# Softplus by absolute value, and the input projections of an attention mixer placed between the quarters of an S5 block

## The chip, the cores and the metric

The kernel runs on one core of one Trainium2 chip. Time is device microseconds of one execution; three runs of the kernel before took 2621.91, 2622.28 and 2622.65 us, and the median of 2622.28 us is what the changed kernel is measured against. One more execution was profiled.

## The reference

Two layers of a streaming encoder are run for 512 prompt rows and 128 sample rows (8 streams of 16 rows), 640 rows of 1024 channels in all. Each layer is FFN, mixer, FFN, each with a LayerNorm. The change lies in the first layer's mixer alone, which joins an S5 state space model with stick-breaking attention:

```python
def sb_block(q_blk, q_pos, k, v):
    z = jnp.einsum('bqhd,bkhd->bhqk', q_blk, k).astype(jnp.float32) * (SB_HEAD_DIM ** -0.5)
    mask = k_pos[None, :] < q_pos[:, None]
    sp = jnp.where(mask, jax.nn.softplus(z), 0.0)
    suffix = lax.cumsum(sp, axis=3, reverse=True) - sp
    w = jnp.where(mask, jnp.exp(jax.nn.log_sigmoid(z) - suffix), 0.0)
    return jnp.einsum('bhqk,bkhd->bqhd', w, v)
...
    proj = x @ w_in              # u | q | k | v, 512 columns each
    ys, h_last = s5_recurrence(u, h0, a_bar, b_bar, c_mat)
    g = jax.nn.gelu(ys + d_skip * u)
    s5_out = g * jax.nn.sigmoid(g @ w_glu + b_glu)
    sb_out = stick_breaking(q, k_all, v_all, offset)
    out = jnp.concatenate([s5_out, sb_out], axis=-1) @ w_out
```

There are 8 heads of 64 channels. The kernel writes k and v and the last S5 state out as well.

## The kernel before

All matrix products of weights run on TensorE (PE) as three products of a value split in a high and a low part (`mm3`, L119). `load_w` brings 512 KB of weights through SyncE's (SP's) queue into one of 4 raw tiles and splits them into two of 11 weight units: ScalarE (ACT) casts (L86), VectorE (DVE) subtracts (L87).

The instructions of each engine stand in a fixed order, which a planner makes when the kernel is built: from the order of the code, from what depends on what, and from when tiles and PSUM banks come free. Each engine takes its list in order and waits at the head of it.

`mixer0` goes like this:

- u is projected for all 640 rows (L119), then four S5 quarters follow, `s5_quarter(j)`. Each is one chain: PE transposes u (L657, L664), multiplies with `m2` (L672) and `tt` (L726); DVE rotates and scans (L680 to L720); PE multiplies the states with `et` (L731), ACT copies `yt` (L733), PE transposes back (L739), DVE copies `y` (L740), then ACT and DVE make the gelu (L743 to L749).
- v is projected (5 row tiles of 24 matmuls of 512 columns). The planner placed these 120 matmuls into the gaps of the four quarters.
- The PSUM banks and the working tiles are handed over from the S5 to attention. DVE and GpSimd (POOL) build the masks (`negc` L795, `negs`).
- `in_qk(p)` projects q and k of a pair of heads p: 4 groups of 24 matmuls, two of 256 and two of 384 columns.
- For each of four pairs, `attend(p, i, ...)` works on block i of the prompt (128 queries against 128(i+1) keys), and `sample(p, ...)` on the 128 sample rows in two halves f. Both go: matmuls to scores z in PSUM, mask added by PE (L837, L882), softplus (L823 to L826), a scan along the keys (L842, L887), z minus the scan (L844, L889), exponential, transposes on PE (L849, L893), a copy (L850, L894), matmuls with v (L853, L902, L906). The result of a pair's prompt blocks is copied at L938, that of its sample block at L916.
- Scores have two PSUM buffers (`bank_z`); `sample` takes one of them, and shares its bank `"o"` and the single tiles `kk`, `tm`, `kc` with the next sample.
- Beside attention stand the projections of pairs 2 and 3, the gate `wglu`, and the first half of the output projection (`out_half(0, t)`, 120 matmuls, accumulated by DVE at L775). The second half, `out_half(4, t)`, needs the last pair and ends the mixer with the LayerNorm.

Of the kernel before, what the change touches and what calls it, by code (L numbers as in the profile page):

```python
# [9 lines left out]
F32 = mybir.dt.float32  # L10
F32R = mybir.dt.float32r
BF16 = mybir.dt.bfloat16
AF = mybir.ActivationFunctionType
ALU = mybir.AluOpType
# [7 lines left out]
T = 640  # L22
TP = 512
NT = 5
KT = 8
NF = 22
HALVES = ((0, 256), (256, 384))
# [8 lines left out]
def kernel(ctx: ExitStack, tc: tile.TileContext, I, O, phases=PHASES):  # L36
    nc = tc.nc

    def pool(name, bufs=1, stack=ctx, **kw):
        return stack.enter_context(tc.tile_pool(name=name, bufs=bufs, **kw))  # L40
# [13 lines left out]
    def bank(k):  # L54
        return pools[k].tile([128, 512], F32, name="bank")

    def bank_a():
        return bank("a")
# [12 lines left out]
    def act_fn(out, in_, func, **kw):  # L71
        if state["preload"] is not None and func in (AF.Exp, AF.Ln):
            with tc.issue_after(state["preload"]):
                return nc.scalar.activation(out, in_, func, **kw)
        return nc.scalar.activation(out, in_, func, **kw)
# [9 lines left out]
    def split(hi, lo, src):  # L85
        nc.scalar.copy(hi, src)  # L86
        return nc.vector.tensor_tensor(lo, src, hi.bitcast(F32), op=ALU.subtract)  # L87

    def raw_tile():
        return pools["raw"].tile([128, 1024], F32, name="raw")  # L90

    def unit(dt=F32R, w=512):
        return pools["w"].tile([128, 1024 // w, w], dt, name="w")

    def load_w(src):

        r = raw_tile()
        nc.sync.dma_start(r, src)
        u = []
        for j in range(2):  # L100
            u.append(unit())
            split(u[j][:, 0], u[j][:, 1], r[:, 512 * j:512 * j + 512])
        return u

    def w_k(w, k):

        c = slice(k % 4 * 128, k % 4 * 128 + 128)
        return w[k // 4][:, 0, c], w[k // 4][:, 1, c]

    def w_j(w, j):  # L110

        return w[j][:, 0], w[j][:, 1]

    def mm3(ps, lhs, rhs):
        n = 3 * len(lhs)
        k = 0
        for (wh, wl), (xh, xl) in zip(lhs, rhs):
            for a, b in ((wh, xh), (wl, xh), (wh, xl)):
                state["pe"] = nc.tensor.matmul(ps, a, b, start=(k == 0), stop=(k == n - 1)).ins  # L119
                k += 1  # L120
# [5 lines left out]
    def cm_proj(w, h, nk=KT, src=None):  # L126
        o, L = HALVES[h]
        s = src or xt
        ps = bank_a()
        mm3(ps[:, :L],  # L130
            [w_k(w, k) for k in range(nk)],
            [(s["hi"][:, k, o:o + L], s["lo"][:, k, o:o + L]) for k in range(nk)])
        return ps
# [464 lines left out]
    def mixer0(ph, last):  # L598
        preload("natural_log_exp_and_others")
        V = nc.vector  # L600
        ctx_m = ExitStack()
        xh, xl = xt["hi"], xt["lo"]
        keep = pool("m0_keep", 1, ctx_m, reuse_waits="tile")
        g_ = [keep.tile([128, T], F32, name=f"g{m}") for m in range(4)]
        vt = keep.tile([128, NT, 512], F32, name="vt")
# [6 lines left out]
        def sigmoid_(t):  # L612

            act_fn(t, t, AF.Ln, bias=1.0)
            act_fn(t, t, AF.Exp, scale=-1.0)


        with ExitStack() as st:
            wk = pool("m0_s5", 1, st, reuse_waits="tile")
# [128 lines left out]
                sigmoid_(g)  # L748
                V.tensor_tensor(g_[j], g, y, op=ALU.mult)  # L749

            for j in range(4):
                s5_quarter(j)


            wv = [load_w(I["m0_v"][i]) for i in range(4)]
            for t in range(NT):
                pv = bank_a()
                mm3(pv, [(xh[:, k, t * 128:t * 128 + 128], xl[:, k, t * 128:t * 128 + 128]) for k in range(KT)],
                    [w_j(wv[k // 2], k % 2) for k in range(KT)])
                nc.scalar.copy(vt[:, t, :], pv)  # L760
                nc.sync.dma_start(O["v"][t * 128:t * 128 + 128, :], vt[:, t, :])
            for r in range(2):
                nc.sync.dma_start(O["s5"][r], fin[:, r])

# [12 lines left out]
        with ExitStack() as st:  # L777
# [42 lines left out]
            nc.scalar.copy(vrev, pr)  # L820

            def softplus_(e, z):
                V.tensor_scalar_min(e, z, 40.0)  # L823
                act_fn(e, e, AF.Exp)
                act_fn(e, e, AF.Ln, bias=1.0)
                V.tensor_tensor(e, z, e, op=ALU.max)  # L826

            def attend(p, i, qT, kT, po):

                n = 128 * i + 128  # L830
                z = bank_z()
                for h in range(2):
                    rows = slice(64 * h, 64 * h + 64)
                    nc.tensor.matmul(z[:, h, :n], qT[rows, n - 128:n], kT[rows, :n],
                                     start=True, stop=False, skip_group_check=True)
                for h in range(2):
                    nc.tensor.matmul(z[:, h, n - 128:n], identb, negc, start=False, stop=True, skip_group_check=True)  # L837
                e = wk.tile([128, 2, 512], F32, name="es", bufs=4)
                S = wk.tile([128, 2, 512], F32, name="S", bufs=2)
                softplus_(e[:, :, :n], z[:, :, :n])  # L840
                for h in range(2):
                    V.tensor_tensor_scan(S[:, h, :n][:, ::-1], onec[:, 0:1].to_broadcast([128, n]),  # L842
                                         e[:, h, :n][:, ::-1], 0.0, op0=ALU.mult, op1=ALU.add)
                V.tensor_tensor(S[:, :, :n], z[:, :, :n], S[:, :, :n], op=ALU.subtract)  # L844
                act_fn(S[:, :, :n], S[:, :, :n], AF.Exp)

                for h in range(2):
                    for j in range(i + 1):
                        nc.tensor.transpose(z[:, h, 128 * j:128 * j + 128], S[:, h, 128 * j:128 * j + 128], ident)  # L849
                nc.scalar.copy(e[:, :, :n], z[:, :, :n])  # L850
                for j in range(i + 1):
                    for h in range(2):
                        nc.tensor.matmul(po[64 * h:64 * h + 64, n - 128:n],  # L853
                                         vt[:, j, 128 * p + 64 * h:128 * p + 64 * h + 64],
                                         e[:, h, 128 * j:128 * j + 128],
                                         start=(j == 0), stop=(j == i), skip_group_check=True)
# [60 lines left out]

            onec = wk.tile([128, 1], F32, name="onec", bufs=1)
            V.memset(onec, 1.0)
            qk = {}  # L920

            def in_qk(p):
                for n, sc in (("q", 0.125), ("k", 1.0)):
                    wt = load_w(I["m0_in"][4 + 2 * p + "qk".index(n)])
                    t = qk[p, n] = keep.tile([128, T], F32, name=n + "T", bufs=4 if n == "q" else 3)
                    for h in range(2):
                        o, L = HALVES[h]
                        nc.scalar.mul(t[:, o:o + L], cm_proj(wt, h)[:, :L], sc)
                nc.sync.dma_start(O["kT"][128 * p:128 * p + 128, :], qk[p, "k"])

            in_qk(0)
            in_qk(1)
            for p in range(4):
                qT, kT = qk[p, "q"], qk[p, "k"]
                po = bank("o")
                for i in range(4):
                    attend(p, i, qT, kT, po)
                V.tensor_copy(qT[:, 0:512], po)  # L938
                sample(p, qT, kT)
                if p < 2:  # L940
                    in_qk(p + 2)
                if p == 1:
                    for m in range(4):
                        split(xh[:, m, :], xl[:, m, :], g_[m])
                    split(xh[:, 4, :], xl[:, 4, :], qk[0, "q"])
                if p:
                    split(xh[:, 4 + p, :], xl[:, 4 + p, :], qT)
# [3 lines left out]
            for h in range(2):  # L951
                o, L = HALVES[h]
# [458 lines left out]
    for ph in phases:  # L1411
        last = ph == phases[-1]
        if ph.startswith("ffn"):
            ffn(int(ph[3]), ph, last, sides.get(ph))
        elif ph == "mix0":
            mixer0(ph, last)
        else:
            mixer1(ph, last)
            if "ffn3" not in phases:
                with ExitStack() as st:  # L1420
                    psum(st, "ssd", a=4, b=4)
                    for _ in ssd_states(pool("ssd", 1, st, reuse_waits="tile")):
                        pass
# [111 lines left out]
```

## Time and profile before

| what | value |
|---|---|
| median of three runs | 2622.28 us |
| the profiled execution, its span | 2621.98 us, 2619.8 us |
| PE busy | 2552.1 us (97%), 15673 matmuls |
| DVE busy | 2028.7 us (77%) |
| ACT busy | 1149.4 us (44%) |
| POOL busy | 238.7 us (9%) |
| mixer 0, from the first S5 transpose to the end of the last sample block | 482.9 to 752.6 us |

Busy PE time holds the latency of pipelined matmuls and is no measure of how full PE is; the waits and the starts of the instructions are. Times in rows of the timeline are microseconds from the start of the span: start, busy time, engine, line, operation, output<-inputs, shape and count; in brackets the idle time of the engine before the row, and what ended it. Rows of groups have count | busy us, mean ns of one | idle before, releaser. Rows of a stretch give its length, then busy time (and count) of PE, of its weight loads, of DVE, ACT and POOL, the granted clock of PE as a share, the share of DMA and GB/s.

### The profile page before, as it was taken

How to read it: one execution, taken by the hardware profiler on the slowest of the kernel's cores; microseconds unless marked ns; L12 is line 12 of the kernel's file. 1: busy time of each engine (PE TensorE's matmuls, PEld its weight loads, DVE VectorE, ACT ScalarE, POOL GpSimd, SP SyncE). 2: the span in 40 equal slices, each digit the busy share in tenths (PEclk: the TensorE clock that was granted, in tenths of full speed). 3: DMA queues.
4: the chain of work that ended last, by engine and by line, in shares of the span. 5: the costliest groups of instructions: out<-in, count | busy, mean ns of one | idle time of the engine just before them, and what ended most of it. 6: DMA issues, size and time to landing. Idle time of an engine off the chain costs nothing. (4 is left out here: it accounts for less than half of the span.)

```text
span 2619.8 us, 41379 instructions
## 1 busy us (share of the span) xinstructions
PE 2552.1 (97%) x15673; PEld 2314.7 (88%) x15673; DVE 2028.7 (77%) x4074; ACT 1149.4 (44%) x2400; POOL 238.7 (9%) x356
## 2 busy tenths in 40 slices
PE   9999999999879999999999999999999999999998
PEld 8999999887559999998999999889989878998887
DVE  8898888657858777767976677777776789887778
ACT  4444444346524344333433343566565553343332
POOL 0000003010030000003000001311111150000001
PEclk9999999999979999999999999999999999999999
DMA  5333234542302233222122222356564622443432
GB/s 180 97 113 100 95 118 138 175 137 91 105 29 65 81 97 97 74 88 81 65 85 88 71 97 99 109 181 183 171 204 131 223 87 94 153 150 125 130 127 91
DMA packets 165751, 302.79 MB, mean 116 GB/s; under 512 B 19072, under 2 KB 89856, under 8 KB 165040
## 3 DMA queue, kind: packets, MB, share of 16 engines
q1 hardware_dynamic: 163792, 293.83, 35.0%
q0 software_dynamic: 1760, 6.33, 0.7%
q8 instruction: 123, 2.02, 0.3%
q14 instruction: 76, 0.62, 0.1%
HBM read 259.56 MB, written 40.54 MB: 115 GB/s over the span
## 5 line engine op out<-in xcount | busy, mean ns | idle before, releaser
L119 PE MATMUL bank<-w,h 128*128 128x512 f32 x2640 | 610.7, 391 | 0.0
L119 PEld LDWEIGHTS bank<-w,h 128*128 128x128 f32 x2640 | 492.3, 188 | 105.3 <-issue 3.4
L119 PE MATMUL bank<-xhi,w 128*128 128x256 f32 (+2 forms) x2528 | 560.4, 313 | 17.9 <-ACT w L86 6.3
L87 DVE TENSOR_TENSOR w<-raw,w 128x512 fp32r<-128x512 f32 x693 | 474.1, 696 | 101.4 <-ACT w L86 99.3
L334 PE MATMUL bank<-xhi,w 128*128 128x320 f32 x2432 | 539.8, 309 | 0.5 <-DVE w L87 0.3
L86 ACT CAST w<-raw 128x512 fp32r<-128x512 f32 x693 | 422.2, 620 | 260.0 <-PE bank L334 131.9
L119 PEld LDWEIGHTS bank<-xhi,w 128*128 128x128 f32 x2528 | 425.0, 190 | 30.7 <-ACT xhi L86 8.5
L334 PE MATMUL bank<-T,w 128*128 128x320 f32 x2736 | 425.1, 309 | 0.0
L334 PEld LDWEIGHTS bank<-xhi,w 128*128 128x128 f32 x2432 | 406.2, 188 | 6.4 <-issue 4.4
L334 PEld LDWEIGHTS bank<-T,w 128*128 128x128 f32 x2736 | 406.5, 188 | 0.0
L119 PE MATMUL bank<-xlo,w 128*128 128x256 f32 (+2 forms) x1264 | 393.4, 312 | 1.8 <-DVE xlo L87 1.8
L334 PE MATMUL bank<-xlo,w 128*128 128x320 f32 x1216 | 375.3, 309 | 0.0
L86 ACT CAST w<-sw 128x512 fp32r<-128x512 f32 x228 | 138.1, 620 | 463.2 <-PE bank L119 275.5
L196 DVE SCALAR_TENSOR_TENSOR yacc<-bank,yacc 128x512 f32<-128x512 f32 x240 | 164.8, 688 | 214.4 <-PE bank L119 212.9
L119 PEld LDWEIGHTS bank<-xlo,w 128*128 128x128 f32 x1264 | 240.8, 191 | 3.4 <-DVE xlo L87 2.4
L334 PEld LDWEIGHTS bank<-xlo,w 128*128 128x128 f32 x1216 | 228.0, 187 | 0.0
L87 DVE TENSOR_TENSOR w<-sw,w 128x512 fp32r<-128x512 f32 x228 | 156.1, 685 | 11.4 <-ACT w L86 11.0
L144 POOL DMA_DIRECT2D w<-in_ln_gb_dram x12 | 6.9, 578 | 1244.1 <-DVE h L87 1224.5
L119 PE MATMUL bank<-w,og 128*128 128x512 f32 x432 | 104.9, 396 | 1.4 <-DVE og L1331 1.2
L119 PEld LDWEIGHTS bank<-w,og 128*128 128x128 f32 x432 | 79.5, 188 | 19.2 <-DVE og L1331 3.1
L86 ACT CAST h<-hf 128x320 fp32r<-128x320 f32 x160 | 73.3, 459 | 49.4 <-DVE hf L371 45.9
L119 PE MATMUL bank<-w,xhi 128*128 128x512 f32 x240 | 83.7, 414 | 1.1 <-DVE yacc L775 1.1
(392 smaller groups left out, 2872.5 us busy)
## 6 DMA issues: line engine op xcount, KB each, us to landing
raw<-in_w_gate_dram SPq DMA_DIRECT2D x88, 512.0 KB, 3.7
raw<-in_w_up_dram SPq DMA_DIRECT2D x88, 512.0 KB, 3.7
raw<-in_w_down_dram SPq DMA_DIRECT2D x88, 512.0 KB, 4.1
raw<-in_m_in_dram SPq DMA_DIRECT2D x52, 512.0 KB, 3.7
raw<-in_m_out_dram SPq DMA_DIRECT2D x24, 512.0 KB, 3.7
csb<-cs_d SPq DMA_DIRECT2D x20, 512.0 KB, 5.2
h<-in_ssd_h_dram SPq DMA_DIRECT2D x16, 512.0 KB, 5.4
h<-in_ssd_h_dram SPq DMA_DIRECT2D x32, 256.0 KB, 2.7
```

The lines of the kernel that those rows point to most:

```text
L86: nc.scalar.copy(hi, src)
L87: return nc.vector.tensor_tensor(lo, src, hi.bitcast(F32), op=ALU.subtract)
L119: state["pe"] = nc.tensor.matmul(ps, a, b, start=(k == 0), stop=(k == n - 1)).ins
L144: nc.gpsimd.dma_start(g_bc[j], bass.AP(tensor=I["ln_gb"].tensor, offset=I["ln_gb"].offset + (2 * n + j) * D, ap=[[0, 128], [1, D]]))
L196: state["acc"] = nc.vector.scalar_tensor_tensor(ya, pb, scale, ya, op0=ALU.mult, op1=ALU.add).ins
L334: nc.tensor.matmul(ps, A[p][:, a, k * 128:k * 128 + 128], B[p][b][:, k, :], start=(first and n == 0), stop=(n == 11), skip_group_check=True)
```

## The change

Softplus was ln(1 + exp(min(z, 40))) and a maximum with z: DVE, ACT, ACT, DVE. It becomes max(z, 0) + ln(1 + exp(-|z|)): ACT three times, then one DVE instruction with two operations.

`in_qk` moves up, and the code now calls q and k of pair 0 after S5 quarter 0, v after quarter 1, q and k of pair 1 after quarter 2. In the last pair `sample` is called ahead of the prompt blocks.

```diff
+            def v_in():
+                wv = [load_w(I["m0_v"][i]) for i in range(4)]
+                ...
+            s5_quarter(0)
+            in_qk(0)
+            s5_quarter(1)
+            v_in()
+            s5_quarter(2)
+            in_qk(1)
+            s5_quarter(3)
-            for j in range(4):
-                s5_quarter(j)
-            wv = [load_w(I["m0_v"][i]) for i in range(4)]
-            ...
             def softplus_(e, z):
-                V.tensor_scalar_min(e, z, 40.0)
-                act_fn(e, e, AF.Exp)
+                nc.scalar.activation(e, z, AF.Abs)
+                act_fn(e, e, AF.Exp, scale=-1.0)
                 act_fn(e, e, AF.Ln, bias=1.0)
-                V.tensor_tensor(e, z, e, op=ALU.max)
+                V.scalar_tensor_tensor(e, z, 0.0, e, op0=ALU.max, op1=ALU.add)
...
-            in_qk(0)
-            in_qk(1)
             for p in range(4):
                 qT, kT = qk[p, "q"], qk[p, "k"]
+                if p == 3:
+                    sample(p, qT, kT)
                 po = bank("o")
                 for i in range(4):
                     attend(p, i, qT, kT, po)
                 V.tensor_copy(qT[:, 0:512], po)
-                sample(p, qT, kT)
+                if p < 3:
+                    sample(p, qT, kT)
```

The order on PE at the last S5 quarter, first before. Rows of L119 are v's projection, L657 and L664 the quarter's transposes, L672 the product with `m2`:

```order
L657 MATMUL bank<-ident,g_4888 80x128 x8
L119 MATMUL bank<-w,xhi 128x512
L119 MATMUL bank<-w,xlo 128x512
L119 MATMUL bank<-w,xhi 128x512 x2
L119 MATMUL bank<-w,xlo 128x512
L119 MATMUL bank<-w,xhi 128x512
L664 MATMUL bank<-ident,ut 128x80 x8
L119 MATMUL bank<-w,xhi 128x512
L119 MATMUL bank<-w,xlo 128x512
L119 MATMUL bank<-w,xhi 128x512
L672 MATMUL bank<-uc,m_5599 64x80 x8
```

The same place now, with the lines of the changed file (L668 for L657, and so on to L750 for L739; L852 is the first score matmul of pair 0, L119 is now q of pair 2):

```order
L668 MATMUL bank<-ident,g_4888 80x128 x8
L675 MATMUL bank<-ident,ut 128x80 x8
L683 MATMUL bank<-uc,m_6012 64x80 x16
L737 MATMUL bank<-tt,uc 80x128 x8
L742 MATMUL bank<-et,hr 80x256 x2
L742 MATMUL bank<-et,hi 80x256
L742 MATMUL bank<-et,hr 80x256
L742 MATMUL bank<-et,hi 80x256 x2
L742 MATMUL bank<-et,hr 80x256
L742 MATMUL bank<-et,hi 80x256
L750 MATMUL bank<-ident,yt 128x80 x8
L852 MATMUL bank<-kT,qT 128x128 x2
```

Nothing of another step stands in the last quarter any more. Behind quarter 0 now stand 59 matmuls of q and k of pair 0 beside the 37 in it, behind quarter 1 96 of v beside 24, behind quarter 2 62 of pair 1 beside 34.

The order on ACT at the first blocks of pair 0, before (L928 copies a projected group, L86 casts weights; `es` are softplus, `S` the exponential, L850 the copy of the transposes):

```order
L928 ACTIVATE kT<-bank 128x384
L86 CAST w<-raw 128x512
L74 ACTIVATE es<-es 128x2x128 x2
L74 ACTIVATE es<-es 128x2x256 x2
L74 ACTIVATE S<-S 128x2x128
L850 COPY es<-bank 128x2x128
```

The same place now (L841 is the absolute value, L625 copies a projected group, L837 is the copy of `vrev`):

```order
L837 COPY vrev<-bank 128x512
L841 ACTIVATE es<-bank 128x2x128
L841 ACTIVATE es<-bank 128x2x256
L74 ACTIVATE es<-es 128x2x128
L74 ACTIVATE es<-es 128x2x256
L74 ACTIVATE es<-es 128x2x128
L74 ACTIVATE es<-es 128x2x256
L625 ACTIVATE qT<-bank 128x384
L86 CAST w<-raw 128x512
L74 ACTIVATE S<-S 128x2x128
```

The two blocks' passes on ACT are now interleaved, three each.

The order on PE at the end of attention, before: the last blocks of pair 3 (L849, L853), then the last sample block from L867 on.

```order
L849 MATMUL bank<-ident,S 128x128 x6
L853 MATMUL bank<-es,vt 64x128 x6
L849 MATMUL bank<-ident,S 128x128 x8
L853 MATMUL bank<-es,vt 64x128 x8
L867 MATMUL bank<-ident,kT 128x128
L870 MATMUL bank<-anti,kk 128x128
L881 MATMUL bank<-kk,qb 128x128
L882 LDWEIGHTS identb
L882 MATMUL bank<-negs,identb 128x128
L884 MATMUL bank<-kc,qb 32x256 x4
```

Now, from the last projection that stands in attention (L119, `out_half(0)`): the end of sample block 2 (L911 to L930), the start of sample block 3 (L885 to L902) and the first scores of pair 3 (L852).

```order
L119 MATMUL bank<-w,xhi 128x512
L911 MATMUL bank<-ident,es 128x128 x3
L920 MATMUL bank<-vrev,tm 128x128
L924 MATMUL bank<-vc,tm 32x128 x8
L930 MATMUL bank<-ident,tm 128x128 x2
L885 MATMUL bank<-ident,kT 128x128
L888 MATMUL bank<-anti,kk 128x128
L899 MATMUL bank<-kk,qb 128x128
L900 LDWEIGHTS identb
L900 MATMUL bank<-negs,identb 128x128
L902 MATMUL bank<-kc,qb 32x256 x4
L852 MATMUL bank<-kT,qT 128x128 x2
```

Sample block 3 stands ahead of pair 3's prompt blocks, beside their first two, and pair 3's last blocks end the list, ahead of the second half of the output projection. No projection stands in pair 3.

More of the change, by code (lines that the diff above doesn't have):

```diff
@@ L615, in sigmoid_, with in_qk @@
             act_fn(t, t, AF.Exp, scale=-1.0)
+        qk = {}
+        def in_qk(p):
+            for n, sc in (("q", 0.125), ("k", 1.0)):
+                wt = load_w(I["m0_in"][4 + 2 * p + "qk".index(n)])
+                t = qk[p, n] = keep.tile([128, T], F32, name=n + "T", bufs=4 if n == "q" else 3)
+                for h in range(2):
+                    o, L = HALVES[h]
+                    nc.scalar.mul(t[:, o:o + L], cm_proj(wt, h)[:, :L], sc)
+            nc.sync.dma_start(O["kT"][128 * p:128 * p + 128, :], qk[p, "k"])
         with ExitStack() as st:
@@ L749, in s5_quarter @@
                 V.tensor_tensor(g_[j], g, y, op=ALU.mult)
-            for j in range(4):
-                s5_quarter(j)
-            wv = [load_w(I["m0_v"][i]) for i in range(4)]
[L756 to L761, printed above, removed]
+            def v_in():
+                wv = [load_w(I["m0_v"][i]) for i in range(4)]
+                for t in range(NT):
+                    pv = bank_a()
+                    mm3(pv, [(xh[:, k, t * 128:t * 128 + 128], xl[:, k, t * 128:t * 128 + 128]) for k in range(KT)],
+                        [w_j(wv[k // 2], k % 2) for k in range(KT)])
+                    nc.scalar.copy(vt[:, t, :], pv)
+                    nc.sync.dma_start(O["v"][t * 128:t * 128 + 128, :], vt[:, t, :])
+            s5_quarter(0)
[5 more added lines that the diff above has]
+            s5_quarter(3)
             for r in range(2):
@@ L919, in mixer0 @@
             V.memset(onec, 1.0)
[L920 to L929, printed above, removed]
-            in_qk(0)
-            in_qk(1)
             for p in range(4):
                 qT, kT = qk[p, "q"], qk[p, "k"]
+                if p == 3:
+                    sample(p, qT, kT)
                 po = bank("o")
```

## The prediction

> **What bounds the kernel now.** I read first the page's slices (its row of granted clock falls below 9 in one place alone, at 720 to 786 us, inside mixer 0), then mixer 0 by stretches, then its timeline engine by engine. The stretches are: the four S5 quarters; q and k of pairs 0 and 1; pair 0's attention; three periods that each run from one pair's copy of its result (L938) to the next; the last sample block.
>
> ```profile
> core 0: us, PE busy (x) PEld busy (x) DVE busy (x) ACT busy (x) POOL busy (x), PEclk, DMA share, GB/s
> 482.88:550.60 67.72, 66.00 (x481) 51.17 (x480) 52.92 (x166) 25.91 (x43) 2.48 (x13) 1.00 0.46 151
> 550.60:578.20 27.60, 27.60 (x188) 26.90 (x186) 9.82 (x21) 10.64 (x20) 6.95 (x22) 1.00 0.52 155
> 578.20:604.16 25.96, 23.75 (x180) 19.36 (x180) 17.85 (x24) 15.21 (x24) 0.00 (x0) 1.00 0.21 63
> 604.16:645.80 41.64, 38.37 (x309) 31.13 (x310) 31.18 (x50) 25.55 (x48) 0.58 (x2) 1.00 0.31 99
> 645.80:686.43 40.63, 37.73 (x254) 26.90 (x253) 36.26 (x63) 28.45 (x54) 0.58 (x2) 1.00 0.25 79
> 686.43:728.88 42.45, 33.62 (x213) 22.15 (x213) 29.41 (x46) 18.92 (x32) 1.76 (x4) 0.85 0.36 112
> 728.88:752.60 23.72, 13.08 (x75) 7.63 (x76) 8.43 (x14) 4.76 (x10) 0.00 (x0) 0.57 0.11 34
> ```
>
> PE is dense and at full clock until about 710 us because projections fill the gaps of attention; at the end nothing fills them, PE is busy 13.08 of 23.72 us and the clock is 0.57. No engine is full in the attention periods (DVE comes closest, 36.26 of 40.63), so they are chains: matmul, softplus, scans, exponential, transposes, copy, matmul. What counts is how long those chains are and what PE does beside them. The rest of the kernel keeps its instructions; I give it no change.
>
> **The change, part by part.** The sum goes from the first S5 transpose (482.88) to the first matmul of the dense output projection (749.93).
>
> (1) *S5.* The rows of one quarter, of the gelu behind the last quarter with the mask behind it, and of the projection rates:
>
> ```profile
> 482.88 1.04 PE L657 MATMUL bank<-ident,g 128*80 128x128 f32 x8
> 497.38 0.72 PE L739 MATMUL bank<-ident,yt 80*128 80x80 f32 x8
> 497.94 1.04 PE L657 MATMUL bank<-ident,g 128*80 128x128 f32 x8
> 549.90 1.39 DVE L740 COPY y<-bank 128x320 f32<-128x320 f32 x2
> 557.99 0.22 DVE L795 CAST negc<-mk 128x128 bf16<-128x128 f32 x1
> 567.30 0.39 ACT L928 ACTIVATE qT<-bank 128x256 f32<-128x256 f32 x1 [1.72 <-PE bank L119]
> 571.46 0.49 ACT L928 ACTIVATE qT<-bank 128x384 f32<-128x384 f32 x1 [1.46 <-PE bank L119]
> 574.18 0.39 ACT L928 ACTIVATE kT<-bank 128x256 f32<-128x256 f32 x1 [1.72 <-PE bank L119]
> 578.98 0.42 DVE L823 TENSOR_SCALAR es<-bank 128x256 f32<-128x256 f32 x1 [1.38 <-PE bank L837]
> 690.43 0.71 PE L119 MATMUL bank<-w,xhi 128*128 128x512 f32 x2
> 694.65 0.63 PE L119 MATMUL bank<-w,xhi 128*128 128x512 f32 x2
> ```
>
> A quarter takes 15.06 us (482.88 to 497.94). 24 matmuls of 384 columns take 4.16 us, of 256 columns 2.72, and one of 512 columns 0.234 (18 start between 690.43 and 694.65). By the order, quarter 0 now holds 37 of pair 0's 96 matmuls and 35 of 384 and 24 of 256 columns stand behind it: 6.1 + 2.7 = 8.8 us. Quarter 1 holds 24 of v's 120, 96 follow: 22.5 us. Quarter 2 holds 34 of pair 1's, 38 and 24 follow: 6.6 + 2.7 = 9.3. Quarter 3 holds none. So the S5 ends at 482.88 + 4 x 15.06 + 8.8 + 22.5 + 9.3 = 583.7. Then the first pair needs its mask, which stands on DVE behind the gelu: 549.90 to 558.21 before, less 0.7 us for a weight split and a qT copy that stood between, 7.6 us from the first y copy, itself 0.3 us ahead of the quarter's end. That is 591.0. Beside it PE has 36 matmuls of pair 2 (4.8 us) and little else. Before, the mask was built under q and k of pairs 0 and 1 (27.6 us, PE full), and the first softplus came at 578.98: **+12.0 us**. Weight loads and splits are as many as before and move with their matmuls; in DVE's and SP's order none stands ahead of quarter 3's work but one kT store and two loads whose buffers are free by then, so I cost them at nothing, covered by the projections behind quarters 0 to 2. Bounds: a bare quarter may be 0.5 us shorter (-2), or be like the mean of four before, 67.72/4 = 16.9 (+7.5).
>
> (2) *Softplus.* 24 passes of DVE (L823) become 24 of ACT:
>
> ```profile
> L823 DVE TENSOR_SCALAR es<-bank 128x384 f32<-128x384 f32 x8 | 4.5, 558 | 13.8 <-PE bank L884 13.8
> L823 DVE TENSOR_SCALAR es<-bank 128x1024 f32<-128x1024 f32 x4 | 4.9, 1218 | 0.3 <-PE bank L837 0.3
> L823 DVE TENSOR_SCALAR es<-bank 128x768 f32<-128x768 f32 x4 | 3.8, 956 | 3.1 <-PE bank L837 3.0
> L823 DVE TENSOR_SCALAR es<-bank 128x512 f32<-128x512 f32 x4 | 2.7, 678 | 0.0
> L826 DVE TENSOR_TENSOR es<-bank,es 128x512 f32<-128x512 f32 x4 | 2.7, 682 | 0.3 <-ACT es L74 0.3
> L196 DVE SCALAR_TENSOR_TENSOR yacc<-bank,yacc 128x512 f32<-128x512 f32 x240 | 164.8, 688 | 214.4 <-PE bank L119 212.9
> L74 ACT ACTIVATE es<-es 128x1024 f32<-128x1024 f32 x8 | 8.5, 1058 | 1.2 <-DVE es L823 1.1
> L74 ACT ACTIVATE es<-es 128x768 f32<-128x768 f32 x8 | 6.7, 843 | 2.9 <-DVE es L823 2.8
> L74 ACT ACTIVATE es<-es 128x512 f32<-128x512 f32 x8 | 5.0, 631 | 2.7 <-DVE es L823 2.2 <-DMA raw<-in_m_out_dram 0.4
> L850 ACT COPY es<-bank 128x1024 f32<-128x1024 f32 x4 | 4.1, 1015 | 4.4 <-PE bank L849 4.4
> 586.38 0.96 DVE L823 TENSOR_SCALAR es<-bank 128x768 f32<-128x768 f32 x1 [1.52 <-PE bank L837]
> 627.41 0.96 DVE L823 TENSOR_SCALAR es<-bank 128x768 f32<-128x768 f32 x1 [1.51 <-PE bank L837]
> 669.15 0.95 DVE L823 TENSOR_SCALAR es<-bank 128x768 f32<-128x768 f32 x1
> ```
>
> DVE loses 4.5 + 4.9 + 3.8 + 2.7 us and four of 0.42 (the 578.98 row): 17.6 us, 4.4 a pair. Abs from PSUM is not in the trace; its bounds are the PSUM copy (1.015) and the old DVE pass (1.218), and I take Exp's 1.058, the same engine and form. The last pass keeps its length: a two-operation add from PSUM (L196, 688 ns) takes what L826 takes (682). So a block still waits for three elementwise steps before its scans, and what counts is who queues behind whom.
>
> Pair 0, from its first pass to that of block 2: 7.40 us before (578.98 to 586.38). ACT now makes Abs, Exp and Ln of block 0 and Abs and Exp of block 1 first, some 3 x 0.42 + 2 x 0.63 = 2.5 us, before DVE can begin; so far ACT worked on block 0 while DVE made block 1's first pass. The rest follows in the old order, since block 2's mask stands on PE behind block 1's transposes; worked to the end it comes to 9.3: +1.9. From there to the pair's copy (17.8, to 604.16) DVE's order had block 3's pass (1.22) between block 2's last pass and its scans; that goes, and 0.96 becomes 0.84: -1.3. **Pair 0: +0.6.** In pairs 1 and 2 the second half (18.4 from 627.41, 16.65 + 0.6 from 669.15) loses the same 1.3. Their first half, with a sample block in it, gains length where ACT is late: casts of g, waiting for the last projections, stand ahead of the sample's last Exp in pair 1 (+0.4), and wglu's exponentials between the passes in pair 2 (+0.9). **-0.9 and -0.4.** Bounds of each: 3 us less, 2 more.
>
> (3) *The last sample block ahead of the last attention.*
>
> ```profile
> 686.43 0.69 DVE L938 COPY qT<-bank 128x512 f32<-128x512 f32 x1 [0.36 <-PE bank L853]
> 690.05 1.03 DVE L823 TENSOR_SCALAR es<-bank 128x384 f32<-128x384 f32 x2 [2.93 <-PE bank L884]
> 708.75 0.96 DVE L823 TENSOR_SCALAR es<-bank 128x768 f32<-128x768 f32 x1
> 728.88 0.69 DVE L938 COPY qT<-bank 128x512 f32<-128x512 f32 x1 [6.24 <-PE bank L853]
> 733.65 0.56 DVE L823 TENSOR_SCALAR es<-bank 128x384 f32<-128x384 f32 x1 [4.08 <-PE bank L884]
> 741.64 0.56 DVE L823 TENSOR_SCALAR es<-bank 128x384 f32<-128x384 f32 x1 [2.04 <-PE bank L884]
> 749.93 0.78 PE L119 MATMUL bank<-w,xhi 128*128 128x512 f32 x1
> ```
>
> Before: sample 2 beside blocks 0 and 1 of pair 3 (22.3 us), blocks 2 and 3 (20.1), sample 3 alone (21.05 to 749.93): 63.5. The two samples share kk, tm, kc and one PSUM bank, so now sample 2 runs without attention, sample 3 beside blocks 0 and 1, and blocks 2 and 3 end it. Nothing is taken out of the chain; one sample changes place. Sample 2: 3.6 to its first pass (686.43 to 690.05), 7.2 and 8.2 for its halves (8.0 and 8.3 in the rows, at the lower clock), 3.0 from there to sample 3's first pass (687.12 to 690.05): 22.0. Sample 3 beside two blocks: 19.5, from 18.7 before (690.05 to 708.75) with bare PE at half clock. Blocks 2 and 3: 17.4, the 20.1 less 1.3 as in the other pairs and less the weight splits and casts that stood between. Bounds: sample 3 no slower than 18.7 and blocks 2 and 3 as fast as pair 2's 16.65 (-1.5), or both as before and sample 2 its 22.3 (+2.2). Sum 58.9: **-4.6**. The projections run out at the end of sample 2, so all of pair 3 is now bare, where before blocks 0 and 1 had cover; the chain is what counts there.
>
> Sum: 12.0 + 0.6 - 0.9 - 0.4 - 4.6 = +6.7 us on the profiled execution's 2621.98 (span 2619.8), which lies 0.3 below the median; carried to the median of 2622.28, **2629.0 us**.
>
> **The rivals.** A: *half clock in quarter 3.* The clock falls where PE is sparse, and after one gap too:
>
> ```profile
> 780.00:790.00 10.00, 7.62 (x51) 7.13 (x50) 10.00 (x16) 6.17 (x10) 6.53 (x4) 0.88 0.34 105
> ```
>
> A PE idle for 2.4 of these 10 us lost 0.12 of the clock, 2.4 us at half rate. Quarter 3 loses the 24 matmuls (5.6 us) that filled a quarter, and has a wait of about 3 us for the rotation on DVE. If one or two stretches of that length or a little more then run at half clock, its matmuls take 2 to 4 us longer: 2632. Against: no clock was lost in the S5 before, where small gaps were many. The Trainium skill (TensorE: Matmul & The Clock Gate, Part 1, the HAM clock gate) says that an idle window of about 3.4 us halves the clock and a busy one restores it. By that rule the sum would be A's 2632 if such a window falls into the quarter, and 2629 if none does.
>
> B: *DVE's relief counts for more.* For it: 36.26 of 40.63. If 2 to 3 us more come off each of three periods: about 2622, no change. Against: ACT, at 28.45 there, gets the same passes.
>
> C (other side): *DVE is the bound of all of attention*, and its 17.6 us come off whole, with 4.6 of the order: 12 - 17.6 - 4.6 = -10: 2612. It decides if DVE always has work waiting when ACT ends its three passes. Against: DVE is idle 10 of 41.64 us in pair 1 and 13 of 42.45 in pair 3.
>
> That the change does not do what it says is left at under 1 in 100: in the new order no table load stands among the softplus passes, and the pass is gone from DVE.
>
> **How the numbers follow.** My forecast 0.55, with its own range 2623 to 2635 (2 us on the S5 and 1 us on each of four chain terms); A 0.12 (2630 to 2639); B 0.20 (2617 to 2626); C 0.13 (2605 to 2617). 0.2% is 5.2 us, about what a measurement of this kernel tells from no change: slower means over 2627.5, faster under 2617.0. Of my forecast 0.40 lies above, 0.15 within; A is all slower; B is 0.17 within, 0.03 faster; C 0.12 faster, 0.01 within. Slower 0.52, same 0.33, faster 0.15. Leaving out C but for its edge, and the ends above, gives 2617 to 2636.
>
> **What would show it.** In the profile after: first softplus at 589 to 593 us; quarter 3 about 15 us with PE idle near half of it; DVE in the three periods lower by 4.4 each and ACT higher by as much, the periods only 0 to 2 us shorter; the dense output projection from about 756. Wrong, if the first softplus comes before 585, or if pair 1's and pair 2's periods fall below 38 us.

## The result and the profile after

The changed kernel takes 2636.14 us (median of four runs, 2632.48 to 2638.88) against 2622.18 of the kernel before on the same chip: 1.0053 times, 95% interval 1.0037 to 1.0069, or 14.0 us slower. Forecast were 2629.0 us (6.7 slower) and a range of 2617 to 2636. The direction was right, the size half of what was measured, and the median lies just above the range. The profiled execution took 2638.88 us, the longest of the four.

Mixer 0 after, by the forecast's stretches (the columns are those of the first fence of the prediction): the S5 up to quarter 3; quarter 3; gelu and mask; pair 0; pairs 1 and 2; and the tail in three, sample 2 alone, sample 3 beside blocks 0 and 1, blocks 2 and 3 up to the dense output projection.

```profile
483.12:568.09 84.97, 83.61 (x577) 71.99 (x576) 51.41 (x142) 30.74 (x53) 2.47 (x13) 1.00 0.46 153
568.09:584.70 16.61, 11.80 (x95) 8.46 (x95) 9.59 (x33) 3.13 (x6) 1.41 (x6) 0.90 0.19 62
584.70:591.94 7.24, 6.76 (x49) 5.69 (x46) 3.96 (x10) 4.29 (x8) 0.30 (x2) 1.00 0.00 0
591.94:620.12 28.18, 23.56 (x177) 19.86 (x176) 15.72 (x26) 17.05 (x28) 4.43 (x15) 1.00 0.29 96
620.12:659.26 39.14, 36.59 (x291) 29.02 (x292) 30.21 (x51) 31.42 (x62) 1.06 (x2) 1.00 0.33 103
659.26:699.12 39.86, 36.76 (x239) 25.09 (x240) 29.50 (x47) 26.61 (x49) 0.58 (x2) 0.96 0.21 68
699.12:723.68 24.56, 21.05 (x133) 13.54 (x133) 13.51 (x22) 9.80 (x20) 1.96 (x4) 0.88 0.56 186
723.68:747.01 23.33, 15.76 (x83) 7.72 (x83) 9.69 (x18) 9.02 (x20) 0.00 (x0) 0.57 0.13 41
747.01:764.87 17.86, 10.42 (x57) 6.79 (x57) 8.51 (x8) 9.24 (x11) 0.00 (x0) 0.50 0.00 1
```

The granted clock, a mean over each stretch, falls below 1.00 in quarter 3, in pair 2 and in sample 2, and is 0.57 and 0.50 through all of pair 3, longer than before. The stretches, read as in the prediction (first softplus pass of pair 0, the copies of the results of pairs 0 to 2, first matmul of the dense projection), in us:

| stretch | before | after | difference | forecast |
|---|---|---|---|---|
| S5 to the first softplus | 96.10 | 108.82 | +12.72 | +12.0 |
| pair 0 | 25.18 | 28.18 | +3.00 | +0.6 |
| pair 1 | 41.63 | 39.14 | -2.49 | -0.9 |
| pair 2 | 40.64 | 39.86 | -0.78 | -0.4 |
| tail | 63.50 | 65.75 | +2.25 | -4.6 |
| sum | 267.05 | 281.75 | +14.70 | +6.7 |

The two spans differ by 17.3 us: these 14.7, 0.2 ahead of the S5, and 2.4 behind. Behind, the dense projection starts at half clock, as it did before, and one more stretch of half clock stands in a later stage (the granted clock is the third column from the end); what else makes up the 2.4 us is open:

```profile
764.87:769.20 4.33, 4.33 (x12) 3.45 (x11) 1.51 (x2) 0.72 (x1) 0.00 (x0) 0.51 0.00 0
2192.40:2195.90 3.50, 3.44 (x11) 3.44 (x12) 3.03 (x8) 0.33 (x1) 0.00 (x0) 0.51 0.00 0
```

Two things stand in the timeline that the forecast had not counted. On DVE, in the first half of pair 0:

```profile
593.80 0.29 DVE L831 TENSOR_TENSOR mk<-mk 128x128 f32<-128x128 f32 x1 [1.62 <-POOL mk L828]
596.66 0.29 DVE L831 TENSOR_TENSOR mk<-mk 128x128 f32<-128x128 f32 x1 [2.31 <-POOL mk L828]
597.13 0.42 DVE L844 SCALAR_TENSOR_TENSOR es<-bank,es 128x256 f32<-128x256 f32 x1
```

The first pair's last softplus step (L844) stands behind the two additions of the sample's mask (L831), and these wait for POOL. Before, POOL built that mask beside q and k of pairs 0 and 1, where nobody waited. POOL began late now:

```profile
591.64 0.20 POOL L824 MEMSET mk<- 128x128 f32 x1 [8.47 <-DVE negc L812]
```

By the profile it had been idle for 8.47 us until DVE cast the first pair's mask (L812), behind the gelu. Both masks are built in the two buffers of the tile `mk`, so most of the second had to wait until the first was read; a third buffer was not tried.

And between sample 2 and sample 3, from the copy of sample 2's result to the first pass of sample 3:

```profile
717.65 0.37 ACT L927 COPY tm<-bank 128x256 f32<-128x256 f32 x1 [1.87 <-PE bank L924]
718.08 0.29 PEld L930 LDWEIGHTS bank<-ident,tm 128*128 128x128 f32 x2 [0.76 <-ACT tm L927]
718.90 0.61 DVE L934 COPY qT<-bank 64x128 f32<-64x128 f32 x2 [1.24 <-PE bank L930]
719.66 0.45 PE L885 MATMUL bank<-ident,kT 128*128 128x128 f32 x1 [0.89 <-DVE qT L934]
722.53 1.08 PE L902 MATMUL bank<-kc,qb 128*32 128x256 f32 x8
723.68 0.49 ACT L841 ACTIVATE es<-bank 128x384 f32<-128x384 f32 x1 [2.10 <-PE bank L902]
```

Sample 3's first transpose (L885) waits for DVE's copies out of the shared bank (L934). The hand-over takes 6.0 us from the start of that copy. The forecast had 3.8 for the same way: its 3.0, and the last 0.8 of the 8.2 for sample 2's second half, which in the rows of before ran from such a copy (749.17) to the dense projection (749.93).

### The profile page after: what moved, and what is told of

Same layout as the page of the kernel before. It is cut to its first block, busy times and chain, and to the rows that moved or that the text cites. A ratio compares the mean times of both kernels' runs of the same rounds, so it can differ in the third digit from the quotient of the medians.

```text
span 2637.1 us, 41403 instructions
## 1 busy us (share of the span) xinstructions
PE 2563.4 (97%) x15673; PEld 2321.4 (88%) x15673; DVE 2016.6 (76%) x4050; ACT 1161.5 (44%) x2424; POOL 242.2 (9%) x356
## 4 chain that ended last, share of the span: by engine, by line
PE 45%; DVE 3%; POOL 1%; DMA 1%; issue 1%; ACT 1%; POOLq 0%; DVEq 0%; SPq 0%; ACTq 0%
PE bank L119 25%; PE bank L334 18%; PE bank L1023 1%; PE bank L1277 0%; PE bank L1301 0%; POOL yacc L165 0%; DVE acc L1115 0%; DMA csb<-cs_d 0%; PE bank L1263 0%; POOL yacc L167 0%; DVE st L155 0%; DMA ext<-z_d 0%; POOL yacc L166 0%; PE bank L1259 0%; PE bank L1234 0%
## 5 line engine op out<-in xcount | busy, mean ns | idle before, releaser
L119 PE MATMUL bank<-w,h 128*128 128x512 f32 x2640 | 610.7, 391 | 0.0
L119 PEld LDWEIGHTS bank<-w,h 128*128 128x128 f32 x2640 | 492.4, 188 | 105.4 <-issue 3.4
L119 PE MATMUL bank<-xhi,w 128*128 128x256 f32 (+2 forms) x2528 | 563.6, 314 | 19.5 <-ACT w L86 6.3
L86 ACT CAST w<-raw 128x512 fp32r<-128x512 f32 x693 | 423.0, 620 | 255.8 <-PE bank L334 131.4
L119 PEld LDWEIGHTS bank<-xhi,w 128*128 128x128 f32 x2528 | 425.6, 190 | 32.4 <-ACT xhi L86 8.6
L119 PE MATMUL bank<-xlo,w 128*128 128x256 f32 (+2 forms) x1264 | 394.0, 312 | 1.3 <-DVE xlo L87 1.3
L86 ACT CAST w<-sw 128x512 fp32r<-128x512 f32 x228 | 138.1, 620 | 463.8 <-PE bank L119 275.4
L119 PEld LDWEIGHTS bank<-xlo,w 128*128 128x128 f32 x1264 | 241.1, 191 | 2.6 <-DVE xlo L87 1.6
L87 DVE TENSOR_TENSOR w<-sw,w 128x512 fp32r<-128x512 f32 x228 | 156.2, 685 | 11.4 <-ACT w L86 11.0
L119 PE MATMUL bank<-w,og 128*128 128x512 f32 x432 | 105.1, 396 | 1.9 <-DVE og L1339 1.0
L119 PEld LDWEIGHTS bank<-w,og 128*128 128x128 f32 x432 | 79.6, 188 | 20.0 <-DVE og L1339 3.5
L86 ACT CAST h<-hf 128x320 fp32r<-128x320 f32 x160 | 73.3, 458 | 49.2 <-DVE hf L371 45.6
L87 DVE TENSOR_TENSOR h<-hf,h 128x320 fp32r<-128x320 f32 x160 | 76.9, 486 | 8.1 <-ACT h L86 7.7
```

## The experiments

All were timed in three rounds beside the kernel before on the same chip; ratios are to that kernel. "After" in a name is the changed kernel. The stretches of all of them, as in the table above, in us:

| kernel | S5 | pair 0 | pair 1 | pair 2 | tail | sum | time, ratio (95%) |
|---|---|---|---|---|---|---|---|
| e1 softplus alone | 96.4 | 24.5 | 39.1 | 40.5 | 63.1 | 263.5 | 2617.85, 0.998 (0.9971 to 0.999) |
| e2 S5 alone | 110.0 | 27.1 | 42.4 | 41.6 | 67.0 | 288.1 | 2644.57, 1.0084 (1.0069 to 1.0099) |
| e3 sample first alone | 96.2 | 25.2 | 41.6 | 40.6 | 66.8 | 270.4 | 2623.75, 1.0005 (0.9996 to 1.0015) |
| e4 after, sample last | 108.7 | 28.2 | 39.1 | 39.9 | 63.9 | 279.9 | 2633.64, 1.0045 (1.0028 to 1.0062) |
| e5 after, mask early | 108.1 | 25.0 | 39.1 | 38.4 | 65.1 | 275.8 | 2639.95, 1.0066 (1.0051 to 1.0081) |
| e6 after, PE kept busy | 107.5 | 29.2 | 39.1 | 38.4 | 59.6 | 273.7 | 2629.62, 1.0027 (1.0017 to 1.0036) |
| e7 after, pair 1 behind quarter 3 | 100.8 | 27.6 | 42.7 | 40.5 | 65.2 | 276.7 | 2631.02, 1.0032 (1.0018 to 1.0046) |
| e8 = e1, PE kept busy | 96.4 | 24.5 | 39.1 | 40.5 | 58.5 | 258.9 | 2612.68, 0.9966 (0.9953 to 0.9979) |
| e9 = e1, projections one pair later | 82.7 | 24.5 | 37.9 | 50.6 | 61.1 | 256.8 | 2608.98, 0.9955 (0.9937 to 0.9972) |
| e10 = e9, PE kept busy | 82.8 | 24.5 | 37.9 | 50.2 | 59.0 | 254.3 | 2609.53, 0.9959 (0.9943 to 0.9975) |
| e11 = e8, sample first | 96.5 | 24.5 | 39.0 | 41.9 | 59.8 | 261.7 | 2613.96, 0.9976 (0.9966 to 0.9986) |

**e1, the softplus alone.** Of the change's diff, only `softplus_`:

```diff
-                V.tensor_scalar_min(e, z, 40.0)
-                act_fn(e, e, AF.Exp)
+                nc.scalar.activation(e, z, AF.Abs)
+                act_fn(e, e, AF.Exp, scale=-1.0)
                 act_fn(e, e, AF.Ln, bias=1.0)
-                V.tensor_tensor(e, z, e, op=ALU.max)
+                V.scalar_tensor_tensor(e, z, 0.0, e, op0=ALU.max, op1=ALU.add)
```

> The kernel before with the new softplus alone. Theory 1 (read from the trace after: pair 1 became 2.5 us shorter, pair 2 0.8, the second half of pair 0 1.2, and the first half of pair 0 would be about 1.2 longer once its 2.9 us wait for the sample mask is left out): the softplus gains, and with pair 3 like pair 2 the time is about 2618, -4 us. Rival (the forecast's terms): +0.6, -0.9, -0.4 and about -1 in pair 3: 2620.5, not to be told from no change.

Measured: 5.1 us faster by the medians (2622.98 before), 3.5 in the profile's sum. Theory 1 has the size, and the rival's 2620.5 lies just outside the interval, which ends at 2620.4. Pair 0's first half is only 0.45 us longer (7.85 against 7.40; theory 1 had 1.2), and pair 1 gains 2.6.

**e2, the S5 order alone.** The change without its softplus and without the sample lines.

```diff
+            s5_quarter(0); in_qk(0); s5_quarter(1); v_in()
+            s5_quarter(2); in_qk(1); s5_quarter(3)
-            for j in range(4): s5_quarter(j)
```

> The kernel before with the new places of q, k and v in the S5 alone. Theory 1: the first score pass comes 12.7 us later as in the changed kernel, and in pair 0 DVE waits for the sample mask that POOL builds, 2 to 3 us more, and one stretch of half clock in quarter 3: 2622.2 + 15 = 2637. Rival: the PE time lost in the S5 is given back later, because projections that were done early leave attention's chain freer: 2630.

Measured: +21.6 us, more than either. 13.9 of it come ahead of the first softplus. The rest is spread, and in the tail (pair 3, then the last sample) the windows show the half clock at work:

```profile
704.94:750.54 45.60, 30.74 (x171) 17.58 (x171) 27.52 (x42) 17.94 (x30) 1.76 (x4) 0.63 0.32 104
750.54:771.96 21.42, 10.77 (x70) 5.70 (x70) 7.07 (x11) 4.04 (x9) 0.00 (x0) 0.50 0.13 37
```

Of these 67.0 us some 55 run at half clock (0.37 of 45.6 lost at half rate is 34, and all of 21.4), against 31 of the 63.5 before. Nothing is given back later, so the rival falls.

**e3, the sample order alone.**

```diff
+                if p == 3:
+                    sample(p, qT, kT)
                 ...
-                sample(p, qT, kT)
+                if p < 3:
+                    sample(p, qT, kT)
```

> The kernel before with the last sample block ahead of the last attention, alone. Theory 1: the order itself costs, since sample 3 now has to wait until sample 2 has handed back its bank (copy, transposes, copies, 2 to 3 us) and the bare stretch at half clock gets longer: +2 to +3 us, 2624.5. Rival (the forecast's term): -4.6 us, 2617.6, and the changed kernel's slow tail comes from its earlier end of the projections and not from this order.

Measured: no difference by the runs (+0.8 us), and in the profiled execution a tail 3.3 us longer. The forecast's -4.6 is excluded by the interval (its lower end is 1.0 us faster); whether it costs 3 us or nothing is not settled by this run.

**e4, the change without the sample order.**

```diff
-                if p == 3:
-                    sample(p, qT, kT)
                 ...
-                if p < 3:
-                    sample(p, qT, kT)
+                sample(p, qT, kT)
```

> The changed kernel with the last sample block behind the last attention again, as before. Theory 1: the order costs 2 to 3 us: 2633.5. Rival: the order gains 4.6 as forecast, and without it the time is 2640.7.

Measured: 10.7 us slower than before, where the whole change is 14.0 slower; the tail is 1.85 us shorter than with the sample first. The rival's 2640.7 is excluded by the interval (its upper end is 2639.2). That the order costs 2 to 3 us is not shown by the times, since the intervals with and without it overlap. With e2 it also says what the softplus is worth behind the new S5 order: 21.6 - 10.7 = 10.9 us, twice its 5.1 alone; what doubles it was not separated.

**e5, the sample's mask ahead of the S5.** The loop that makes `negs` moves from the start of attention to the start of the S5's working pool:

```diff
         wk = pool("m0_s5", 1, st, reuse_waits="tile")
+            negs = keep.tile([128, 2, 128], BF16, name="negs", bufs=1)
+            for half in range(2):
+                ...
+                V.tensor_scalar(negs[:, half], ms[0], -1.0, 1e30, op0=ALU.add, op1=ALU.mult)
```

> The changed kernel with the sample mask (negs) built by POOL and DVE ahead of the S5. Theory 1: pair 0's first half took 11.55 us instead of the forecast 9.3 because DVE's list has the mask's two additions, which wait for POOL until 593.8 and 596.7, ahead of the first softplus add; with the mask out of the way that half falls to about 8.7, 2.9 us less in all: 2633. Rival: ACT's six passes in a row set it; at most 1 us comes off: 2635.5.

Measured: in its place as theory 1 has it, 8.40 us from the first pass to block 2's instead of 11.55, and L844 waits for ACT alone:

```profile
598.38 0.42 DVE L844 SCALAR_TENSOR_TENSOR es<-bank,es 128x256 f32<-128x256 f32 x1 [1.79 <-ACT es L74]
```

But the time rose to 2639.95 us. The S5 now starts at 488.24 instead of 483.12, and the mask is now built in the last LayerNorm of the stage ahead; three rows there, POOL's mask (L640) around its small LayerNorm step (L158), and DVE, which waits for that step:

```profile
461.77 0.55 POOL L158 TENSOR_TENSOR rs<-rs,mhalf 128x1 f32<-128x1 f32 x1
462.36 1.29 DVE L171 SCALAR_TENSOR_TENSOR yacc<-yacc,rs,w 128x1024 f32<-128x1024 f32 x1 [0.56 <-POOL rs L158]
462.55 2.84 POOL L640 TENSOR_SCALAR_AFFINE_SELECT mk<-mk 128x128 f32<-128x128 f32 x3
```

The wait was real and worth 3.2 us; the place chosen for the mask costs more than that. A stretch of half clock also fell there (0.83 from 460 to 470 us, 1.00 in the changed kernel), and how the 5.1 us divide was not tried. Behind the first dense matmul this execution is also 4.0 us longer than the changed kernel's, which the mask doesn't explain.

**e6, PE kept busy in pair 3.** Behind the first half of the output projection:

```diff
             for t in range(NT):
                 out_half(0, t)
+            for _ in range(40):
+                nc.tensor.matmul(bank_a()[:, :256], kk3[:, 0], vt[:, 0, :256], start=True, stop=True)
```

Here `kk3` is sample 3's tile `kk`, so that none of them can start ahead of sample 3; the product goes to a PSUM bank that nothing reads.

> The changed kernel with 40 matmuls of 256 columns more (ident times v, never read) in the gaps of pair 3, where no projection is left. Theory 1: half clock in the bare pair 3 costs much of the missed 6.9 us of the tail; at full clock the last sample beside blocks 0 and 1 falls from 23.3 to about 20, the blocks 2 and 3 from 18 to 16, and the extra matmuls give 1 to 2 us of it back: 2632. Rival: the chain there is made of ACT and DVE steps and semaphore latency, PE's clock hardly matters, and the extra matmuls only stand in the way: 2637 or more.

Measured: 2629.62 us, 6.5 less than the changed kernel by the medians (1.0027 for 1.0053). The tail's three windows:

```profile
696.61:720.60 23.99, 20.77 (x135) 13.43 (x135) 13.51 (x22) 9.81 (x21) 1.97 (x4) 0.96 0.57 192
720.60:740.67 20.07, 20.03 (x133) 14.37 (x133) 9.58 (x18) 9.25 (x19) 0.00 (x0) 0.88 0.16 48
740.67:756.18 15.51, 13.50 (x86) 10.09 (x86) 8.42 (x8) 9.24 (x10) 0.00 (x0) 1.00 0.00 0
```

DVE and ACT do nearly the same work (9.58 and 9.25 us, 8.42 and 9.24), PE does more, and the stretches fall from 23.33 to 20.07 and from 17.86 to 15.51. So the clock was the cost: 6.2 us of the tail. Pair 2 is also 1.4 us shorter in this execution, without the half-clock stretch that it had; e5, which has no extra matmuls, shows the same 38.4 us there at clock 1.00, so they have no part in that.

**e7, q and k of pair 1 behind quarter 3.**

```diff
             s5_quarter(2)
-            in_qk(1)
             s5_quarter(3)
+            in_qk(1)
```

> The changed kernel with q and k of pair 1 called behind quarter 3, so that its 96 matmuls fall into quarters 2 and 3 and none stands between them. Theory 1: the cost of the S5 part is the PE time left empty (quarter 3 bare, 62 matmuls behind quarter 2): the first softplus comes 8 us earlier, the time is 2628. Rival: a quarter with projections in it takes longer (16.8 against 15.1 us), and what is done earlier is missing as cover later: 2632 to 2636.

Measured: the first softplus comes 8.05 us earlier, as theory 1 has it. Quarters 2 and 3 now have projections in their gaps:

```profile
542.96:557.49 14.53, 14.02 (x124) 11.79 (x123) 11.13 (x40) 3.74 (x8) 0.96 (x5) 1.00 0.68 216
557.49:575.80 18.31, 17.83 (x147) 15.29 (x146) 14.13 (x40) 7.70 (x13) 1.41 (x6) 1.00 0.25 93
```

Quarter 2 takes 14.5 us, and the y copy of quarter 3 comes 17.1 us after its start, against 16.0 when it was bare and lost some clock, and 14.7 when it was bare at clock 1.00 (e6): the rival's price is 1.1 to 2.4 us. The time falls by 5.1 us only, since pair 1 takes 42.7 instead of 39.1; what lengthens it was not tried.

**e8, e1 with PE kept busy** (45 matmuls of the same size, `ident` in place of `kk3`, behind `out_half(0, t)`).

> The kernel before with the new softplus and 45 matmuls of 256 columns more (ident times v, never read) behind the first half of the output projection, in the gaps of pair 3's last blocks and of the last sample block. Theory 1 (half clock costs there): the clock stays 1.0 from 715 to 746 us, PE's busy time there halves, and about 5 us come off 2617.9: 2613. Rival (the clock does not matter, extra matmuls stand in the way): 2618 to 2622.

Measured: 2612.68 us, 5.2 less than e1 by the medians. The tail of e1 and then of e8 (pair 3, then the last sample):

```profile
683.26:725.07 41.81, 34.39 (x220) 23.09 (x220) 26.20 (x41) 22.26 (x38) 1.76 (x4) 0.88 0.37 114
725.07:746.34 21.27, 10.77 (x70) 5.69 (x70) 5.95 (x9) 5.02 (x11) 0.00 (x0) 0.50 0.12 38
```

```profile
682.91:723.08 40.17, 39.40 (x255) 27.40 (x256) 26.19 (x41) 22.26 (x38) 1.75 (x4) 1.00 0.38 119
723.08:741.41 18.33, 17.95 (x125) 13.25 (x126) 5.95 (x9) 5.02 (x11) 0.00 (x0) 1.00 0.14 44
```

The same chain, with clock 1.00 for 0.50: 18.33 for 21.27 us. The kernel before had this cost too; the forecast's rows of its tail were rows at half clock.

**e9, all projections one pair later** (on e1).

```diff
             in_qk(0)
-            in_qk(1)
             for p in range(4):
                 ...
-                if p < 2:
-                    in_qk(p + 2)
+                for n in ((1,), (2, 3), (), ())[p]:
+                    in_qk(n)
```

> The kernel before with the new softplus, and with q and k of pair 1 called behind sample 0 and those of pairs 2 and 3 behind sample 1, so that all projections move back by one pair: only pair 0's stand between the S5 and attention, and the output projection's first half reaches into pair 3 and the first half of sample 3. Theory 1 (what counts is where PE's cover lies; bare stretches cost most, at half clock): 13.8 us less ahead of attention, which pairs 0 to 3 take up again but for the part that fills the bare 30 us of pair 3: 2606 to 2612. Rival: the chain gets longer, since sample 1 now runs ahead of pair 2's blocks instead of beside them (some 8 us): 2614 to 2618.

Measured: 2608.98 us, 13.0 less than the kernel before on that chip and the fastest of all. Ahead of attention 13.7 us go, pairs 0 and 1 take no longer than in e1, and both theories show in the rows of pair 2 and of the rest:

```profile
626.56:677.19 50.63, 44.90 (x320) 35.76 (x321) 36.28 (x61) 38.12 (x75) 1.77 (x2) 0.93 0.28 90
677.19:716.29 39.10, 37.85 (x246) 25.86 (x247) 26.60 (x41) 21.71 (x37) 0.58 (x2) 1.00 0.18 55
716.29:738.25 21.96, 14.20 (x91) 8.64 (x92) 10.92 (x17) 8.37 (x17) 1.17 (x2) 0.76 0.44 156
```

Pair 2 takes 10.1 us more, since sample 1 runs ahead of it (the rival), and pair 3 runs at clock 1.00.

**e10, e9 with PE kept busy at its end** (16 such matmuls).

> As the last, with 16 matmuls of 256 columns (never read) in the gaps left at the end of sample 3. Theory 1: the last bare 10 us run at full clock, 1 to 2 us less than the last one. Rival: too short to matter, or the extra matmuls stand in the way: the same or 1 us more.

Measured: 2609.53 us, not to be told from e9. The tail is 2.0 us shorter and the sum 2.5, but the time does not follow; that is no verdict for either.

**e11, the sample order at full clock** (e8 with the lines of e3).

> The kernel before with the new softplus, the last sample block ahead of the last attention, and 45 matmuls never read in the gaps behind the first half of the output projection: beside e8 (2612.7, sample last) the order of the sample alone, at full clock. Theory 1 (the order gains nothing even at full clock, because sample 3 waits 2.5 us longer for sample 2's hand-over than the forecast's 3.0 us): tail 59 to 60 us against 58.5, time 2613 to 2615. Rival (the forecast's -4.6 holds at full clock): tail 54, time 2608.

Measured: 2613.96 us and a tail of 59.8 against e8's 58.5. Without any half clock in the tail the order still gains nothing: theory 1. The hand-over from sample 2 to sample 3 takes 5.2 us here. The tail's three parts, sample 2 alone, sample 3 beside blocks 0 and 1, and blocks 2 and 3:

```profile
684.26:707.09 22.83, 22.67 (x149) 15.53 (x151) 13.52 (x22) 9.09 (x19) 1.75 (x4) 1.00 0.43 126
707.09:726.35 19.26, 18.89 (x136) 13.09 (x137) 10.78 (x20) 9.57 (x21) 0.00 (x0) 1.00 0.42 140
726.35:744.07 17.72, 15.94 (x99) 12.31 (x99) 9.59 (x10) 9.96 (x11) 0.00 (x0) 1.00 0.00 0
```

## Why the forecast was too low

- **The S5 term (+12.0) was right:** +12.7. Quarter 0 with its 8.8 us took 23.8, quarter 1 with 22.5 took 37.1, and from quarter 3's y copy to the first softplus pass went 7.9 us for 7.6. Rival A happened once, on top: the clock was halved in quarter 3 (0.90 over the window), and from its first transpose to its y copy it took 15.96 us against 14.88 of quarter 0, and 14.66 of the same bare quarter at clock 1.00 in e6: 1.3 us.
- **The softplus term was right in kind, wrong in two sizes.** The step that failed in pair 0 is "the rest follows in the old order; worked to the end it comes to 9.3": it was 11.55, because the sample's mask on POOL lost its cover with q and k, and stands ahead of L844 on DVE. e5 took 3.15 us off there. I had costed only the first pair's mask. The other size is pair 1's: -2.5 for -0.9, in the change as in e1 (-2.6), a part of what rival B priced.
- **The tail (-4.6) failed: +2.25, 6.85 us off.** Step by step: sample 2 alone 24.56 for 22.0, nearly all from the hand-over (6.0 for 3.8, as above; in "3.0 from there to sample 3's first pass" I left out the copies L934 out of the shared bank; at clock 1.00 it takes 5.2, in e11). Sample 3 beside blocks 0 and 1 23.33 for 19.5, and blocks 2 and 3 17.86 for 17.4. I wrote that the projections now run out at the end of sample 2, and that "the chain is what counts there"; but PE's matmuls are links of that chain, and e6 shows them 6.2 us slower at half clock. "19.5, from 18.7 with bare PE at half clock" allowed 0.8 us for it. In blocks 2 and 3 the loss doesn't show against the forecast, since the rows that I took them from were at half clock already. The kernel before, blocks 2 and 3 of pair 3 and then sample 3 alone:

```profile
708.75:728.88 20.13, 11.46 (x71) 7.70 (x69) 13.86 (x17) 9.34 (x11) 1.17 (x2) 0.68 0.34 114
728.88:749.93 21.05, 10.41 (x69) 5.50 (x70) 7.07 (x11) 4.04 (x9) 0.00 (x0) 0.58 0.12 38
```

So the step that failed is the term (3) itself. At clock 1.00 the forecast's parts are nearly right (e11, with the extra matmuls in it: 22.8, 19.3 and 17.7 us for 22.0, 19.5 and 17.4), but at clock 1.00 the old order is no longer either (e8: 58.5 in all, for 59.8). The -4.6 came from setting parts priced near full clock against rows of which 31 of 63.5 us ran at half clock. It was the price of the clock and not a gain of the order, and in the changed kernel the half clock stayed.

- With PE kept busy (e6) the sum is 273.7, +6.7 on before, the forecast's very number. That is partly chance: its terms are +11.4, +4.0, -2.5, -2.2 and -3.9, and the mask and the hand-over are in it, set off by the softplus gaining more than forecast. Of the 8.0 us between the two sums 6.2 lie in the tail, where the extra matmuls stand; 1.4 each in the S5 and in pair 2, and -1.0 in pair 0, go with single stretches of half clock that fell elsewhere in that execution.
- Rival C (DVE the bound everywhere) is out: e1, which takes the same 24 passes off DVE, gains 5.1 us of 17.6.

So the loss is the S5 order: alone it costs 21.6 us (e2), while the softplus alone gains 5.1 (e1) and the sample order alone shows no difference (e3). Placing the projections early empties PE where the last quarter and then pair 3 stand. The first place pays most, 12.7 us up to the first softplus. In the tail the half clock cost 6.2 us (e6), but 4.6 of that kind were there without the early placing too (63.1 in e1, 58.5 in e8). e9 does the opposite, moving them later, and is the fastest together with e10.

## What to carry to other kernels

Work that fills an engine's gaps is a fixed stock: ask where a move takes it from, up to the end of the stage, not only where it puts it. Where a move leaves a stretch of small matmuls bare, price that stretch at half clock, and look whether the rows that you scale are at half clock themselves. When cover is moved away, list everything that it hid, on every queue: here it was also a mask that POOL builds for something needed much later.

## What the runs showed of the hardware that was not expected

The clock stayed at half although PE, by its busy times in the profile, was hardly idle. In the changed kernel's pair 3, where the record of the granted clock gives 0.5 from 738.4 to 769.1 us:

```profile
739.05 0.79 PE L920 MATMUL bank<-vrev,tm 128*128 128x128 f32 x2 [0.94 <-DVE tm L912]
739.77 1.08 PE L924 MATMUL bank<-vc,tm 128*32 128x128 f32 x16
740.78 1.65 PE L852 MATMUL bank<-kT,qT 64*128 64x384 f32 x2
...
747.16 1.12 PE L871 MATMUL bank<-es,vt 128*64 128x128 f32 x8 [0.46 <-ACT es L868]
748.21 2.08 PE L852 MATMUL bank<-kT,qT 64*128 64x512 f32 x4
```

From 739.05 to 750.63 PE idles once, for 0.46 us, and in these 11.6 us the clock does not rise. The Trainium skill (TensorE: Matmul & The Clock Gate, Part 1, the HAM clock gate) says that about 3.4 us of sustained work restore the full clock; the trace does not agree for this kind of work, matmuls that use 64 rows or 32 columns of the array among transposes (the ends of matmuls in the profile are modelled, so PE may have been less busy than the rows say). Nor does it take an idle stretch of that length to lose the clock: in quarter 3 the one long wait was 2.65 us.

```profile
577.39 1.41 PE L742 MATMUL bank<-et,hr 128*80 128x256 f32 x4 [2.65 <-issue]
```

What the records do show is that every stretch of half clock lasts 3.41 us or a multiple of it, but for the one that the program's end cuts, as the same section of the Trainium skill has the window. Within one execution they also begin a whole number of 3.413 us apart. Which gaps are hit differs between executions: quarter 3 was hit in the changed kernel and not in e6, though both issue the same work there. Counting such windows on from the recorded stretches, the wait of 2.65 us lies inside one window in the changed kernel, behind which the clock is halved, and is cut in two by a boundary at 575.20 in e6 (the first row is of the changed kernel, the others of e6):

```profile
574.56:577.97 3.41, 0.76 (x5) 0.48 (x4) 3.41 (x12) 0.00 (x0) 0.00 (x0) 1.00 0.01 2
571.78:575.20 3.42, 2.25 (x25) 1.92 (x20) 3.25 (x9) 0.00 (x0) 0.00 (x0) 1.00 0.01 2
575.20:578.61 3.41, 1.62 (x7) 0.98 (x8) 3.34 (x17) 0.00 (x0) 0.00 (x0) 1.00 0.00 0
```

PE's busy time in the window does not decide it alone: in e2 the clock is halved behind a window with 1.93 us busy (569.58 to 572.99), and in e6 it stays behind one with 1.62.
